# A branch prefetch hint for TensorE's loop in an 8192 x 8192 fp32 transpose

## The chip, the cores and the metric

One core of one Trainium2 chip. The metric is device time in microseconds. The kernel before takes 1264.06 us (median of six runs, 1263.41 to 1265.18).

## The reference

```python
def setup_inputs():
    return {"x": np.random.randn(8192, 8192).astype(np.float32)}

def reference(x: np.ndarray) -> np.ndarray:
    return np.transpose(x)
```

It moves 268 MB in and 268 MB out, and computes nothing.

## The kernel before

x is cut into 128 blocks of 128 rows by 4096 columns (2 MB each). A block is loaded into one of three buffers; TensorE transposes it in 32 pieces of 128 x 128 into four PSUM tiles; ScalarE and VectorE copy those into nine output buffers; ScalarE's queue stores full buffers and issues the next load. TensorE's program is a loop: three blocks per turn, 43 turns. The condition at the head exists because 128 is not a multiple of three: the first turn has only two blocks. Every other engine's program is written out without a loop.

```python
        def transposes(k):
            nc.tensor.sem_inc(s_ld[k], -16).wait_op(s_ld[k], 16, "sem-ge")        # line 110: block landed
            for h in range(NR // 2):
                if h < 2:
                    n = NR // 4
                    nc.tensor.sem_inc(s_bank[h], -n).wait_op(s_bank[h], n, "sem-ge")  # line 114: PSUM free
                for b in range(2 * B):
                    ...
                    tr = nc.tensor.transpose(...)                                  # line 117
                tr.then_inc(s_pe, 1)
        ...
        with nc.Fori(0, T // NIN + 1, engines=pe) as turn:                         # line 132
            with nc.tensor.If(turn > 0):                                           # line 133
                transposes(NIN - 1)
            for k in range(NIN - 1):
                transposes(k)
```

## Time and profile before

| | before |
|---|---|
| time, median | 1264.06 us |
| share of the 16 DMA engines taken by the two data queues | 98.8% + 1.2% |
| TensorE: matmul busy, idle before matmuls | 742.7 us, 493.1 us |
| a taken backward branch | 211 ns |
| end of the loop head to the first step after the landing of the block it waits for | 5.9 us median, 0.78 us at the tightest |

The first row of shares says what is full, the second what has room, and the last two set the cost of the branch against the room in front of it. The lines behind the table stand in the prediction.

### The profile page before, as it was taken

To read this page: it belongs to the slowest core of one execution; us is meant where nothing else is said; L and a number is where in the kernel's file an instruction comes from. 1 tells how busy PE (TensorE), PEld (TensorE's weight loads), DVE (VectorE), ACT (ScalarE), POOL (GpSimd) and SP (SyncE) were. 2 spreads that over 40 slices of the span, in tenths; PEclk is the share of its full clock that TensorE was granted. 3 is DMA by queue.
4 is the path that set the end of the run, shared out by engine and by line. 5 is a ranking of instruction groups with operands and counts; after the bars stand their busy time and mean duration, and the time that the engine had idled before them with its cause. 6 is when DMAs were issued, how large, how long until landed. Compare 5 with 4: busy or idle time off the path is not lost. (4 is left out here: it accounts for less than half of the span.)

```text
span 1262.9 us, 9961 instructions
## 1 busy us (share of the span) xinstructions
PE 742.7 (59%) x4096; PEld 721.8 (57%) x4096; DVE 316.1 (25%) x311; ACT 263.0 (21%) x321; POOL 0.7 (0%) x6
## 2 busy tenths in 40 slices
PE   6565565665566555655566655666565655656561
PEld 5565555665566555655565655656565645655561
DVE  3322222222222222222222222222222222222220
ACT  3212121222122211212221121121212211122120
POOL 0000000000000000000000000000000000000000
PEclk9967768677777777686766687777868687777865
DMA  9999999999999999999999999999999999999998
GB/s 381 429 430 420 429 431 428 430 429 431 428 430 430 431 428 429 430 430 430 426 425 414 429 430 429 430 430 430 428 430 430 431 428 430 430 430 429 430 427 339
DMA packets 39274, 536.98 MB, mean 425 GB/s; under 512 B 4320, under 2 KB 4832, under 8 KB 6240
## 3 DMA queue, kind: packets, MB, share of 16 engines
q10 hardware_dynamic: 38832, 530.60, 98.8%
q1 hardware_dynamic: 432, 6.29, 1.2%
q14 instruction: 9, 0.07, 0.0%
q8 instruction: 1, 0.02, 0.0%
HBM read 268.44 MB, written 268.44 MB: 425 GB/s over the span
## 5 line engine op out<-in xcount | busy, mean ns | idle before, releaser
L117 PE MATMUL ps<-ident,in 128*128 128x128 f32 x4096 | 742.7, 364 | 493.1 <-PEq L114 493.1
L117 PEld LDWEIGHTS ps<-ident,in 128*128 128x128 f32 x4096 | 721.8, 219 | 513.9 <-issue 513.6
L208 DVE COPY regs<-ps 128x1024 f32<-128x1024 f32 (+1 forms) x311 | 316.1, 1034 | 921.2 <-PE ps L117 704.5
L208 ACT COPY regs<-ps 128x1024 f32<-128x1024 f32 (+1 forms) x320 | 261.7, 843 | 973.6 <-PE ps L117 654.9
L208 ACT ACT_TABLE_LOAD x1 | 1.3, 1283 | 0.9 <-SPq L69 0.9
L86 POOL TENSOR_SCALAR_AFFINE_SELECT ident<-ident 128x128 f32<-128x128 f32 x1 | 0.3, 293 | 0.2 <-POOL ident L84 0.2
L84 POOL MEMSET ident<- 128x128 f32 x1 | 0.2, 204 | 0.5 <-SPq L69 0.5
L241 POOL MEMSET const-bfloat16-1.0<- 128x1 bf16 x1 | 0.1, 102 | 0.0
L241 POOL MEMSET const-uint8-127<- 128x1 uint8 x1 | 0.1, 102 | 0.0
L241 POOL MEMSET const-float32-0.0<- 128x1 f32 x1 | 0.1, 99 | 0.2 <-issue 0.2
L241 POOL MEMSET const-float32-1.0<- 128x1 f32 x1 | 0.1, 99 | 0.0
## 6 DMA issues: line engine op xcount, KB each, us to landing
in<-in_x_dram ACTq DMA_DIRECT2D x125, 2048.0 KB, 22.5
out_dram<-regs ACTq DMA_DIRECT2D x114, 2048.0 KB, 18.4
out_dram<-regs ACTq DMA_DIRECT2D x4, 1792.0 KB, 17.5
in<-in_x_dram SPq DMA_DIRECT2D x3, 2048.0 KB, 11.6
out_dram<-regs ACTq DMA_DIRECT2D x4, 1536.0 KB, 15.1
out_dram<-regs ACTq DMA_DIRECT2D x4, 1280.0 KB, 16.7
out_dram<-regs ACTq DMA_DIRECT2D x4, 1024.0 KB, 16.6
out_dram<-regs ACTq DMA_DIRECT2D x4, 768.0 KB, 16.4
```

What stands on the lines that cost most here:

```text
L84: nc.gpsimd.memset(ident, 0.0).then_inc(s_id, 1)
L86: nc.gpsimd.affine_select(out=ident, in_=ident, compare_op=mybir.AluOpType.not_equal, fill=1.0, base=0, pattern=[[-1, P]], channel_multipl ...
L117: tr = nc.tensor.transpose(pss[h][:, b * P:(b + 1) * P], ins[k][:, j:j + B * P - B + 1:B], ident,)
L208: cp = nc.scalar.copy(out=o, in_=i) if e == 0 else nc.vector.tensor_copy(out=o, in_=i)
L241: nc = _bacc.Bacc("TRN2", target_bir_lowering=False, num_devices=1)
```

## The change

The change aims at a wait for code at the loop's backward branch. A hint at the head of each turn, naming the loop's closing branch as likely taken, was meant to take it away. The whole diff:

```diff
-        with nc.Fori(0, T // NIN + 1, engines=pe) as turn:
+        with nc.Fori(0, T // NIN + 1, engines=pe, hint_back_edge=True) as turn:
```

In the built program it is one instruction more on TensorE (BRANCH_PREFETCH_HINT, 43 times), the first of each turn; no other engine's program differs.

## The prediction

> **What bounds the kernel now.** I read the page first, then the busy time by stages of the span, then the lines of TensorE's control instructions, the order of time around one backward branch, and last the semaphore and packet records of the trace.
>
> The head of the page and its parts 2, 3 and 5 say who is full:
>
> ```profile
> span 1262.9 us, 9961 instructions
> PE 742.7 (59%) x4096; PEld 721.8 (57%) x4096; DVE 316.1 (25%) x311; ACT 263.0 (21%) x321; POOL 0.7 (0%) x6
> ...
> DMA  9999999999999999999999999999999999999998
> GB/s 381 429 430 420 429 431 428 430 429 431 428 430 430 431 428 429 430 430 430 426 425 414 429 430 429 430 430 430 428 430 430 431 428 430 430 430 429 430 427 339
> ...
> q10 hardware_dynamic: 38832, 530.60, 98.8%
> q1 hardware_dynamic: 432, 6.29, 1.2%
> q14 instruction: 9, 0.07, 0.0%
> q8 instruction: 1, 0.02, 0.0%
> ...
> L117 PE MATMUL ps<-ident,in 128*128 128x128 f32 x4096 | 742.7, 364 | 493.1 <-PEq L114 493.1
> ```
>
> The reader is to see three things. The two data queues take 98.8% + 1.2% of the 16 DMA engines' time, the rate is 425 to 431 GB/s in nearly every slice, and no slice between the first and the last is idle: the kernel is a copy of 537 MB at the full rate, and 537 MB / 430 GB/s = 1249 us is already 99% of the span. TensorE, by contrast, is idle for 493 us, and every microsecond of that idle time ends at its own sequencer, which waits for a semaphore (the line named, 114, is the second wait of a block; the first, on line 110, is the one for the loaded block of x). And the last two rows are instruction fetches: ten packets in the span, one of them of 16 KiB and nine of 8 KiB, no more.
>
> The stages agree. Between 35 and 1200 us the DMA share is 1.01 in each stretch while TensorE is busy for 59 to 61% of it, although its granted clock is only 0.73 to 0.77:
>
> ```profile
> 35.00:300.00 265.00, 156.04 (x875) 151.52 (x875) 67.83 (x65) 55.27 (x61) 0.00 (x0) 0.77 1.01 428
> 300.00:600.00 300.00, 180.34 (x987) 175.31 (x985) 76.36 (x73) 63.29 (x77) 0.00 (x0) 0.74 1.01 430
> ```
>
> Now the branch itself. The lines of TensorE's loop (132) and of the condition at its head (133) read:
>
> ```profile
> L132 PEldq MOVE  x44: 29/29/39, 1.7 to 1203.3; - x44
> L132 PEldq ALU_OP  x43: 36/36/42, 16.9 to 1232.2; - x43
> L132 PEldq COMPARE_BRANCH  x43: 79/211/218, 17.0 to 1232.3; - x43
> L133 PEldq COMPARE_BRANCH  x43: 77/77/222, 1.9 to 1203.4; - x43
> ```
>
> The columns are minimum, median and maximum in ns. There are 43 turns, so 42 taken backward branches; the one of 79 ns is the last, which falls through. A taken branch costs 211 to 218 ns, all 42 alike. None shows microseconds of waiting for code. Where the loop's records are complete, the loop's add to the MOVE that opens the next turn is 0.37 to 0.42 us.
>
> Where that lies in time is seen around one branch, here the one at 321.3 us:
>
> ```profile
> 318.13 6.55 PE L117 MATMUL ps<-ident,in 128*128 128x128 f32 x32 [3.42 <-PEq L114]
> ...
> 327.88 5.27 PE L117 MATMUL ps<-ident,in 128*128 128x128 f32 x32 [3.19 <-PEq L114]
> ```
>
> The sequencer runs ahead of the array: it branches at 321.29 us, while the 32 transposes that started at 318.13 still run until 324.68. It then stands at the wait for the next block from 321.72 until 327.62 us, when that block lands. So the branch is over 5.9 us before anyone could use it.
>
> I measured this for every turn from the trace's records. From the end of the condition at the head of a turn to the end of the wait for the block there are 5.9 us in the median, 5.8 us at least from the seventh turn on, and 0.78 us at the tightest (the second turn, at 17 us, while the pipeline fills; the first turn has 6.1, the third 4.2). And from the last part of a block's landing to the sequencer's next step it takes 0.028 to 0.029 us for all 128 blocks, the 43 behind a loop head and the 85 in the middle of a turn alike. **The loop head delays no block at all today.**
>
> [...] a turn is 3 x 32 weight loads, as many matmuls, 9 semaphore steps, 1 move, 1 add and 2 branches, some 205 instructions by the trace's records. [...] one 16 KiB packet in the whole span, at 20.1 us, not 42 of them. [...]
>
> **The change part by part.** The built program of after differs from that of before on TensorE alone, by one instruction: a prefetch hint as the first of each turn, naming the loop's closing branch as likely taken. DVE, ACT, GpSimd and SP have the same rows in the same order.
>
> 1. *Removed:* nothing from the program. What it might save is a fetch stall at the 42 taken branches. Before has none to save: 42 x 0 = 0. At the very most it could shorten a taken branch from 211 to the 79 ns of one not taken, 42 x 0.13 = 5.5 us of sequencer time, all of it inside waits of 0.78 us or more: 0 of the span.
> 2. *Added:* 43 hints. No row shows one; as an estimate I take it to lie between a MOVE (29 ns, with its slot about 0.09 us from start to the next start) and a taken branch (0.21 us). 43 x 0.1 to 0.2 = 4 to 9 us of sequencer time. Each stands between the branch and the wait for the block, where 0.78 us is free in the tightest turn and 5.8 in most: 0 of the span. The first hint comes at about 1.8 us, the first block at 8.2: hidden too.
> 3. *Moved:* the body slides by one instruction slot[...].
> 4. *At the end:* the last hint runs at about 1203 us. The last block lands at 1228.9, is transposed, copied and stored, and the last data packet ends at 1261.2. No loop head lies in that tail.
>
> Sum: 0 us, and 1264.5 us stays.
>
> **The rivals.**
>
> *The hint makes traffic.* If it fetches its target's block every turn[...], that is 43 x 16 KiB = 0.70 MB more on engines that are full. At 430 GB/s it costs 1.6 us: 1266.1. In favour: the transfers are the bound, so any added byte does count. [...] It would be seen as about 43 more 16 KiB packets. Even then it is 0.13%.
>
> [...] The only 16 KiB fetch of before took 0.93 us as a packet. As an estimate, two or three such times per stall, about 2 to 3 us, fit into the 5.8 us of wait at the loop head. A stall in the middle of a block of 32 is less free: TensorE is idle 3.2 to 4.5 us per block of 9.76 us, and lateness there delays the copies, the free banks and the stores. Yet nine output buffers and three input blocks stand between that and an idle DMA queue. I make it 1264 to 1272 us if it occurs, with a chance of perhaps 3%.
>
> *TensorE becomes the bound.* It would need 3 us or more added to each of 128 blocks; the change touches 43 of them by 0.2. Ruled out.
>
> *A real saving.* It needs a stall at the branch now, and the 211 ns of all 42 and the 0.028 us of every wake-up speak against it. Under 1%.
>
> **How range and chances follow.** The mechanism gives 0 and the likeliest miss +1.6 us. The three runs of before spread over 1.2 us[...]. So I give 1261.5 to 1268.0, a little more room above than below. Two per cent is 25 us: a slowdown of that size needs 0.6 us lost on each of 43 turns out of a wait of 5.8 us, or the transfers hurt in a way that the profile gives no hint of. [...] So 97% within, 2% slower, 1% faster.
>
> **What would show it right or wrong.** In the profile of after: the backward branch still 211 ns, or somewhat shorter, without effect; the add-to-MOVE distance longer by 0.05 to 0.2 us for the hint; the wait for the block shorter by just that, still above 5 us in most turns; the wake-up still 0.028 us; DMA share 98.8% and 425 GB/s; instruction packets still about ten (fifty would be the first rival). The prediction is wrong if the wake-up or the blocks' period of 9.76 us grows, if 16 KiB packets appear each turn together with gaps among the data packets, or if matmuls of one block show a hole of a microsecond or more that before doesn't have.

The forecast's sum is 0 us removed, 0 added and 0 in the tail, so that 1264.5 us stays. The second rival is a stall that the hint brings where before has none.

## The result, and the profile after

The changed kernel takes 1266.04 us (median of six runs, 1265.38 to 1272.13), before 1264.06 in the same rounds. The ratio is 1.0021, 95% interval 1.0003 to 1.0038: the same within 2%, and in these rounds a little slower. (A ratio is the mean time of one kernel's fast runs over that of the other's of the same rounds, so it is not quite the ratio of the medians.) The kept trace of after is of its longest run, 1272.13 us; for sizes I therefore also use a second trace of the same program, of a run of 1265.97 us (run e2_hint below).

The head, the queues and TensorE's group, from the page of after:

```profile
span 1269.9 us, 10004 instructions
PE 744.8 (59%) x4096; PEld 723.9 (57%) x4096; DVE 316.0 (25%) x311; ACT 263.0 (21%) x321; POOL 0.7 (0%) x6
...
q10 hardware_dynamic: 38832, 530.60, 98.6%
q1 hardware_dynamic: 432, 6.29, 1.2%
q14 instruction: 9, 0.07, 0.0%
...
L117 PE MATMUL ps<-ident,in 128*128 128x128 f32 x4096 | 744.8, 364 | 497.4 <-PEq L114 497.4
```

There are 43 instructions more, one per turn. The DMA engines are as full as before and TensorE idles as much. One row is gone: q8, the single 16 KiB instruction packet that before has at 20.1 us. In the packet records it now starts at 1270.9 us, after the span's end (and at 1265.3 in the second trace). The records don't say which code a packet holds.

The loop's own lines in the trace of after, in ns as minimum/median/maximum:

```profile
L132 PEldq BRANCH_PREFETCH_HINT  x43: 31/31/45, 1.8 to 1210.4; - x43
...
L132 PEldq COMPARE_BRANCH  x43: 80/216/225, 16.3 to 1239.4; - x43
L133 PEldq COMPARE_BRANCH  x43: 85/85/250, 2.1 to 1210.6; - x43
```

A hint takes 31 ns. The taken branch got no shorter: 216 ns against 211. From the loop's add to the next turn's first move it is now 0.465 us in the median against 0.371, so a hint costs the sequencer 0.094 us. And the order of time around one branch, now at 322.1 us, again TensorE alone:

```profile
318.94 5.52 PE L117 MATMUL ps<-ident,in 128*128 128x128 f32 x32 [4.49 <-PEq L114]
328.76 5.57 PE L117 MATMUL ps<-ident,in 128*128 128x128 f32 x32 [4.30 <-PEq L114]
```

The array still idles for more than 4 us, until the next block has landed. From the end of the loop head to the sequencer's first step after that landing it is 5.88 us in the median (before 5.93), and that step still comes 0.028 to 0.029 us after the landing (the wake-up), for all 128 blocks. So at the loop head nothing was gained and nothing lost. What is left to explain is a difference of 2 us in 1264, and the packet that moved.

### The profile page after: what moved, and what is told of

The parts are those of the page before. It is cut to its first block, busy times and chain, and to the rows that moved or that the text cites. A ratio compares the mean times of both kernels' runs of the same rounds, so it can differ in the third digit from the quotient of the medians.

```text
span 1269.9 us, 10004 instructions
## 1 busy us (share of the span) xinstructions
PE 744.8 (59%) x4096; PEld 723.9 (57%) x4096; DVE 316.0 (25%) x311; ACT 263.0 (21%) x321; POOL 0.7 (0%) x6
```

## The experiments

The theory: the transfers set the time; the branch stalls nowhere, its cost lies inside waits, and a hint has nothing to save. The rivals: the hint or the shift of the code by one slot (an instruction's place in the program) costs time by itself; the moved packet does; or 2 us is what two loads of a program onto a chip differ by.

### Is the 2 us there at all: the same program twice, and the changed one again

e1_same is the kernel before, unchanged.

> The kernel before, unchanged, as a kernel of its own: it measures how far two loads of the same program differ. The theory that the 2 us between after and before are what loads or runs of a program differ by expects a ratio to before anywhere from 0.998 to 1.002, and above 1.001 would support it. The theories that the hint or the shifted slot costs 2 us expect 1.000 within 0.0005. All expect the one 16 KiB instruction packet at about 20 us.

1264.39 us against 1264.22; ratio 0.9999, interval 0.9985 to 1.0013. The packet came at 19.5 us. Between two loads of the kernel before there is no difference clear of noise.

e2_hint is the changed kernel.

> The changed kernel once more, on this chip. If the hint or the shifted slot costs 2 us, the ratio to before is again 1.001 to 1.002 (1265.5 to 1266.5 us); if it was variation of loads or runs, it may be 0.999 to 1.001 and lie within the unchanged kernel's own spread. The 16 KiB instruction packet is expected again at the end of the program instead of at 20 us, since it went there in the first trace of after.

1266.58 us against 1264.22; ratio 1.0019, interval 1.0006 to 1.0033, and the packet after the end again. The same size in another session: no luck of one load, it seemed.

e12_hint is the changed kernel a third time, on another chip than e2_hint.

> The changed kernel a third time, as the control on this chip. If the 2 us belong to it: 1.001 to 1.002 and the packet at the end. If they were luck of two earlier loads: 1.000 within 0.0006.

1265.08 us against 1264.5; ratio 1.0005, interval 0.9991 to 1.0018. No 16 KiB packet stands in its trace at all, neither in the span nor after it. So the difference isn't steady: 0.21%, 0.19% and 0.05% in three sessions. All have the same sign, but the last is not clear of zero, and by the mark set before the run (1.000 within 0.0006) it speaks for luck of the two earlier loads.

### Is it the hint, its place or the slot?

e3_move was to put a register move where after has its hint:

```diff
+            nc.regs_mov(spare, 0)
```

> The kernel before with one register move at the head of each turn, where after has its hint: the same shift by one slot and nearly the same sequencer time (a move takes 29 ns, the hint 31 ns), no hint. If the shift or the added time costs the 2 us: ratio 1.001 to 1.002. [...]

(Otherwise a ratio of 1.000 was expected.)

1264.1 us, ratio 1.0000 (0.9987 to 1.0014). But this run tells nothing about the shift. Its trace has 9961 instructions, as many as before, and no row for the move's line: the compiler had dropped a move that nobody reads. It is one more run of the kernel before.

e4_late moves the hint from the head of a turn to its end (the loop is written out by hand for that, here cut):

```diff
+            at = nc.tensor.mark_branch_hint_location()
             nc.regs_alu(i, i, 1, op=mybir.AluOpType.add)
+            nc.tensor.br_lt(i, T // NIN + 1, ...).branch_hint(at)
```

> The hint moved from the head of a turn to its end, just ahead of the add and the branch. [...] the packet comes back at about 20 us here, and if that move costs the 2 us the ratio is 1.000. If hints as such cost 2 us, the ratio is 1.001 to 1.002 as for the hint at the head. If the packet comes at the end here too, the place of the hint in the turn does not matter to it.

1265.26 us, ratio 1.0006 (0.9993 to 1.002), with one run of 1270.51 among its five. The packet is back inside the loop, at 20.6 us. So with a hint at the head of each turn the packet stays away (1270.9 us in after, 1265.3 in e2_hint), and with one at the end it does not. On the time the run is inconclusive.

Three runs then put the hint in a condition, all with the same instructions at the same slots, so that only the turns in which it runs differ:

```diff
+            with nc.tensor.If(turn == 1):        # e9_only1;  e10_not1: turn != 1;  e11_all43: turn < 64
+                at = nc.tensor.mark_branch_hint_location()
```

> One hint instead of 43: it stands in a condition and runs in the second turn alone, which is the turn in which the kernel before fetches its 16 KiB block at 20 us. If the moved packet and what follows from it in the first 35 us is the cause of the 2 us (my theory), the packet is missing at 20 us here too and the ratio is 1.001 to 1.002. If it is a cost of each hint (rival: 43 hints at some 45 ns each), one hint costs nothing: 1.000, within 0.0006, whatever the packet does.

One hint: 1263.91 us against 1264.1, ratio 0.9999 (0.9985 to 1.0012). The packet came at 56.8 us: neither at 20 nor missing, which I had not foreseen. My theory, that its absence at 20 us costs the 2 us, missed: it was absent there, and nothing was lost.

> The reverse: 42 hints, in every turn but the second. If the moved packet is the cause, the packet stays at 20 us and the ratio is 1.000, within 0.0006. If each hint costs, 42 of them cost what 43 do: 1.001 to 1.002. A result between would mean that neither accounts for it alone.

42 hints: 1264.17 us, ratio 0.9999 (0.9985 to 1.0013); the packet at 34.8 us, where 20 was expected. That is in the third turn, which is hinted, 1.9 us after the backward branch of the one turn that is not. In e9_only1 it stayed away from the second and the third turn, though only the second is hinted, and came 0.6 us after the branch into the fourth. So the turn in which a hint runs is not simply the turn that has no packet; the rule stays open.

> The same program as the last two with single hints left out, but with the condition always true: 43 hints, each behind one more branch, at the same slots. The run with 42 of them cost nothing, so a cost of each hint expects 1.000 here. If the cost goes with the 16 KiB packet not coming inside the loop, then either the packet is at the end again and the ratio is 1.001 to 1.002, or it is inside the loop and the ratio is 1.000; packet at the end with a ratio of 1.000, within 0.0006, would break that link.

43 hints: 1265.36 us against 1264.5, ratio 1.0006 (0.9993 to 1.002); the packet after the end, at 1265.0 us. That is at the edge of the mark that was to break the link between packet and 2 us (1.000 within 0.0006), and its interval still holds 1.001 to 1.002: the link is not confirmed.

What follows: a hint as such, and the shift by some slots, cost nothing that can be seen: 42 hints, with the condition around them, are within 0.15% (1.9 us) of none. And whether the 16 KiB packet comes inside the loop depends on the turns that are hinted: e10_not1 (34.8 us) and e11_all43 (1265.0 us) differ in one turn's hint alone. The two states side by side, the queue rows of e10_not1:

```profile
span 1260.7 us, 10046 instructions
...
q14 instruction: 9, 0.07, 0.0%
q8 instruction: 1, 0.02, 0.0%
```

and of e12_hint, where the row q8 is missing as in after:

```profile
span 1265.2 us, 10004 instructions
...
q14 instruction: 9, 0.07, 0.0%
```

The place of that packet does show in the time, though not for all of it. Each run gives its whole time and the span from the program's first to its last instruction; the rest is start and end outside the program:

| kernel | 16 KiB packet | time minus span, mean (range), us |
|---|---|---|
| before (9 runs beside e9_only1) | 20 us | 2.16 |
| e4_late | 21 us | 2.16 (2.11 to 2.20) |
| e10_not1 | 35 us | 2.15 (2.11 to 2.17) |
| e9_only1 | 57 us | 2.15 (2.11 to 2.18) |
| e8_big_hint (below) | five, all inside the span | 2.15 (2.13 to 2.16) |
| after (7 runs) | after the end | 2.27 (2.16 to 2.51) |
| e2_hint | after the end | 2.49 (2.09 to 3.07) |
| e11_all43 | after the end | 2.61 (2.12 to 3.26) |
| e12_hint | none in the trace | 2.30 (2.18 to 2.40) |

Where the packet stays out of the loop, 0.1 to 0.45 us is added outside the program, in some runs a whole microsecond (the packet itself takes 0.93 us in before and 1.2 us in after); where it is inside, nothing. This goes with the packet in all rows, and in single runs too: in the traces of after, e2_hint and e11_all43 the packet ends 2.2, 3.3 and 3.5 us behind the last instruction, and their time exceeds the span by 2.23, 3.07 and 3.23 us. That with a hint at the head of every turn of three blocks the packet does not come before the program's end is shown (1270.9, 1265.3 and 1265.0 us; in e12_hint it is missing); that the end waits for it now and then is a guess that fits all of this, but no run moved the packet without a hint to test it.

The rest of the difference lies inside the span: the median span of e2_hint is 1264.0 us against 1262.1 for before beside it, but that of e12_hint is 1262.8 against 1262.3. I found no stall to go with it. In no trace of hinted kernels do the weight loads within a group of eight lie more than 0.3 us apart, no block is taken up later than 0.029 us after it landed, and between 35 and 1200 us the DMA share of e2_hint, e11_all43 and e12_hint is 1.01 in every stage. The landings of the blocks show where it arises: between the tenth block (73 us) and the 25th (220 us), the traces of after, e2_hint, e11_all43 and e12_hint, all those without a 16 KiB packet in the span, lose 1.6 to 3.5 us against the trace of before (up to there they were 1.3 to 2.0 us ahead of it), and the seven other traces of kernels without an added delay that were laid beside it, one run each, lose none. The DMA share is 1.01 in that stage as in before, so the same bytes took the engines longer; why is not shown.

The cause of this part, 0.4 to 1.9 us, stays open; at its small end it is no more than what e7_big, which has no hint, differs from before the other way. The two long runs (1272.13 and 1270.51 us), each the first of a hinted kernel, have another shape: their blocks land every 9.82 us in the median, those of the other traces every 9.76 us. The reason is open as well; the first runs of e2_hint and e12_hint were not as long.

### Where a hint might have had something to save: a turn of 1210 instructions

The loop of before has some 205 instructions per turn. Here it has 18 blocks of x per turn instead of three:

```diff
-        with nc.Fori(0, T // NIN + 1, engines=pe) as turn:
-            with nc.tensor.If(turn > 0):
-                transposes(NIN - 1)
-            for k in range(NIN - 1):
-                transposes(k)
+        TURN = 18
+        with nc.Fori(0, T // TURN, engines=pe):          # e8_big_hint: hint_back_edge=True
+            for k in range(TURN):
+                transposes(k % NIN)
+        for k in range(T % TURN):
+            transposes(k % NIN)
```

> No hint, [...] 18 blocks of x per turn, 7 turns and 2 blocks after them, some 1210 instructions per turn against 205. [...] each of the 6 taken backward branches would wait for a fetch[...], and 16 KiB packets would come in every turn[...]. [...] 5 or 6 such packets in all and 0.2 us per branch. The time stays within 0.2% of before in both cases, since a turn's head is free for 5.8 us.

(These are two cases that exclude each other: the wait and the packets in every turn, or neither.)

1263.44 us against 1264.1, ratio 0.999 (0.9975 to 1.0006). Its backward branches and its instruction packets:

```profile
q8 instruction: 5, 0.08, 0.0%
...
L133 PEldq COMPARE_BRANCH  x7: 76/208/223, 154.6 to 1212.2; - x7
```

The five 16 KiB packets start at 28.6, 50.4, 86.4, 126.1 and 1222.6 us: four in the first turn, which ends at 154.6, one behind the loop, none in the six turns between. All six taken branches cost 207 to 223 ns. Even in a turn six times as long no 16 KiB packet comes after the first turn, and its branches take as long as those of before (211 to 218 ns).

> The same loop of 1210 instructions with the hint at the head of each turn. If the loop without it stalls at its branches, the hint takes those 6 stalls away (branch to next instruction back at 0.2 to 0.3 us), yet the time is the same as without it within 0.2%: the stall was hidden. If the loop without it doesn't stall, nothing changes but perhaps the place of the packets.

1265.29 us, ratio to before 1.0002 (0.9985 to 1.0018). Against e7_big, the same loop without the hint in the same session, its mean is 1.6 us longer (0.13%; four runs each, and their ranges overlap), all of it inside the span. The branch is a little longer here as well:

```profile
L133 PEldq COMPARE_BRANCH  x7: 88/223/249, 154.2 to 1211.7; - x7
```

Again five packets, one of which moved from 126.1 us to 1227.6, behind the loop. So I found no loop in which the hint saved anything. A turn of more than 1210 instructions was not tried.

### How much delay the loop head takes

Two runs without a hint let TensorE turn an empty inner loop at the head of each turn:

```diff
+            with nc.Fori(0, 13, engines=pe):             # e6_delay10: 26
+                pass
```

> No hint; instead TensorE turns an empty inner loop of 13 turns at the head of each turn, an estimate of 4.5 to 5 us (0.35 to 0.38 us per turn, from the measured distance of the add to the next turn's first move). My theory: the head of a turn is free for 5.8 us, so the ratio is 1.000 within 0.001, although this is some 50 times a hint's time. If TensorE were on the path that sets the end, 43 x 4.7 us would make it 16% slower.

The delay measured 4.7 us per turn, 202 us in all. The time: 1264.35 us against 1264.5, ratio 1.0005 (0.999 to 1.0021). Only three blocks of 128 were taken up more than 0.03 us after they landed, all while the pipeline fills: the two behind the second and third loop head, 4.6 and 1.7 us late, and one in between, 0.3 us. From the fourth turn on there is none, and by block 20 the trace stands where the one of before does, to 0.1 us.

> The same with 26 inner turns, an estimate of 9 to 10 us, beyond the free 5.8 us: every third block of x is transposed some 4 us late. Loads are under way for 22.5 us and come every 9.76, so more than two are queued: if that queue takes the lateness up, the ratio is 1.000 to 1.005. If the slack at the head is all there is, 43 x 4 us = 170 us: ratio 1.13.

The delay measured 9.45 us. The time: 1279.47 us, ratio 1.012 (1.0104 to 1.0135), so 15 us and neither 6 nor 170. The busy time of the stages says where. Columns are the stretch and its length, busy time of PE, PEld, DVE, ACT and POOL, granted clock, DMA share and GB/s. First before, then e6_delay10:

```profile
0.00:35.00 35.00, 22.51 (x158) 21.62 (x159) 11.54 (x17) 11.43 (x20) 0.70 (x6) 1.00 0.96 389
35.00:65.00 30.00, 16.19 (x115) 15.54 (x115) 8.77 (x10) 7.67 (x14) 0.00 (x0) 0.93 1.01 427
65.00:300.00 235.00, 139.85 (x762) 135.97 (x761) 59.06 (x55) 47.60 (x48) 0.00 (x0) 0.75 1.01 428
```

```profile
0.00:35.00 35.00, 14.61 (x86) 14.19 (x87) 5.64 (x9) 6.65 (x11) 0.70 (x6) 0.90 0.81 322
35.00:65.00 30.00, 19.28 (x140) 18.39 (x139) 11.00 (x16) 9.57 (x17) 0.00 (x0) 0.89 0.91 361
65.00:300.00 235.00, 123.78 (x768) 119.41 (x768) 60.35 (x57) 48.56 (x51) 0.00 (x0) 0.78 1.01 423
```

In the first 65 us the DMA engines run dry: (389 - 322) x 35 + (427 - 361) x 30 us, divided by 430, is 10 us of transfers not made. The third row adds (428 - 423) x 235 / 430 = 3 us. After that the transfers are nearly as full as before, although every third block of x is still transposed 3.7 us (median) after it landed: blocks land every 9.76 us in the median in both kernels. By the 31st block the trace lies 12.7 us behind that of before, by the last 15.6. So in the steady state most of the lateness beyond the free time is taken up (loads are under way for 22.3 us in the median and land every 9.76, so more than two are queued), and the start, with a DMA share of 0.81 and 0.91 against 0.96 and 1.01, pays for 10 of the 15 us; the last 3 us, added in steps later, were not traced to a cause.

## Why the prediction was right

*The bound.* Right. Transfers fill the DMA engines after as before, and e5_delay5 is the strongest evidence: 202 us of added TensorE time, 50 times what the 43 hints take, left the time where it was.

*"Removed: 42 x 0 = 0".* Right. The branch did not get shorter; it went from 211 to 216 ns. That it could shorten toward the 79 ns of a branch not taken was given as the utmost, and it did not happen in after, in e2_hint (216 ns) or in e8_big_hint (223 ns against 208).

*"Added: 43 x 0.1 to 0.2 = 4 to 9 us of sequencer time, 0 of the span".* The size was at the lower edge: 0.094 us a turn, 43 x 0.094 = 4.0 us. That it is hidden is right: the wake-up stayed at 0.028 to 0.029 us in every turn.

*"Moved: the body slides by one instruction slot".* What the step drew from that was not shown. It looked only at the loop's own code, and the 16 KiB packet went from 20.1 us to 1270.9, after the end. The prediction's forecast of "still about ten" instruction packets held; it missed that one of them changes its place.

*The rivals.* The traffic rival made 1266.1 us, and 1266.04 was measured. That is a coincidence: it asked for about 43 more packets, and the trace has not one more. The rival of a new stall did not occur either; no block shows a hole (within a group of eight, the weight loads lie at most 0.3 us apart). TensorE did not become the bound, and there was no saving.

*The signs of being wrong.* One of them did appear in the kept trace of after: the blocks' period grew, from 9.762 to 9.825 us. It belongs to that long run and not to the hint as such: in e2_hint and e12_hint, the same program, it is 9.763 and 9.762. The other signs stayed away.

*The range.* 1261.5 to 1268.0 held the median, and a little more room above was the right side. The point forecast of 1264.5 was 1.5 us low: the sum of 0 left out about 2 us, for which no term of it stands. The width of the range rested in part on a spread of executions that no run had shown; the nine runs of before beside e9_only1 have since given 1263.43 to 1267.69 us, 0.34%. Of what the changed kernel takes more than before, 0.1 to 0.45 us goes with the packet's late place; the remainder is not explained.

*A limit of the argument.* The prediction's sum used the free time at the loop head alone, though it named the buffers as further room. e6_delay10 shows that room: in the steady state, most of the lateness beyond it is absorbed too (3.7 us on every third block, the blocks' period still 9.76 us), and the tight place is the start, not the turns in the middle.

## What to carry to other kernels

Before adding a hint to a loop, look for the stall it is to remove: the longest taken branch in the trace, and the instruction packets per turn. Here, in before and e7_big, the taken branches took 207 to 223 ns, and no 16 KiB packet came in the loop after its second turn. Shortening them was not seen; what was seen with the hint was one packet in another place, with 0.1 to 0.45 us more outside the program where that place was past its end or the packet was missing. What a change inside a wait is worth was read here from a delay of known size at the same spot: 4.7 us a turn, within the 5.9 us of room, left the time where it was (ratio 1.0005), and 9.45 us cost 1.2%. One such run tells whether the room is there; when two kernels differ by 0.2%, repeat both on other chips before explaining it, and check that a control's extra instruction is in its trace.
